# Feed-forward products of a decoder layer in a seven-product scheme, the down projection taken once for all tokens

## The chip, the core and the metric

One core of a Trainium2 chip runs the whole program. The metric is the time of one execution on the device in microseconds (us). TensorE (PE in the rows; PEld is its weight load) multiplies, VectorE (DVE), ScalarE (ACT) and GpSimd (POOL) work on elements, and SyncE (SP) issues every DMA transfer of this kernel.

## The reference

One layer for 2048 tokens of 1024 channels in float32: a token mixer, then a feed-forward block with 2816 hidden channels. Cut to what matters here:

```python
h = rmsnorm(x, norm_mix_in) * (1.0 + sc1) + sh1
q, k, v, p, u, vg = jnp.split(h @ w_in, SPLITS, axis=-1)
merged = jnp.concatenate([rmsnorm(stick_breaking_attention(q, k, v), mn[:512]),
                          rmsnorm(multiscale_pool(p), mn[512:768]),
                          rmsnorm(chunked_spatial_gating(u, vg), mn[768:])], axis=-1)
x = x + g1 * (merged @ w_out)
h2 = rmsnorm(x, norm_ffn_in) * (1.0 + sc2) + sh2
gate, up = jnp.split(h2 @ w_gate_up, 2, axis=-1)
x = x + g2 * ((jax.nn.silu(gate) * up) @ w_down)
return rmsnorm(x, final_norm)
```

The attention has 8 heads of 64 channels and looks back over 512 tokens; sc1, sh1, g1 and the like come from a conditioning vector through `w_ada`.

## The kernel before

The tokens go in four groups of 512. Every large product is made of float32 operands that are cut in a high and a low half (`a = a_hi + a_lo`, both in the format fp32r), and three products hi*hi, hi*lo and lo*hi (`mm3`) are added in PSUM. So 128 input channels by 128 output channels for 512 tokens are three matmuls with 512 columns. Cutting a weight tile (`wsplit`) costs an ACT copy and a subtraction on DVE or POOL.

- `proj_a(g)` and `proj_b(g)` make q, k, v, the pooling and the gating channels of group g. q, k and v go to scratch in DRAM.
- `attention()` is a generator. For each group and head it loads k, q and v back, and for each of four tiles of 128 queries `att_front` makes the weights: a score matmul into the PSUM tile `z`, a copy and three activations on ACT, a maximum, a prefix sum (`TENSOR_TENSOR_SCAN`) and a subtraction on DVE, masks on POOL, and the last Exp on ACT. `att_back` transposes the weights of a pair of tiles in three rounds through the one PSUM tile `tr`, cuts them (ACT, then DVE, into `wT`) and multiplies with v into `av`. After the second pair of a head, `av` goes out through a tile of its own tag (`av`, one buffer).
- `out_proj(g)` multiplies with `w_out` and adds g1 times that to x; `h_ffn(g)` transposes the normed rows into channels.
- `gate_up` makes 128 hidden channels at a time for one group: 24 matmuls for gate, 24 for up, each into one bank of the three-bank PSUM tag `d`, then the sigmoid on ACT and DVE. `down` (through `tok_gemm`) takes four hidden tiles at a time, for each of four token tiles and two halves of the channels: 12 matmuls into a bank, a DVE multiplication by g2 and a POOL addition into the rows of x held in SBUF.

The feed-forward weights are so read and cut once for each group, four times in all. The order comes from generators: `weave(fg, *sides)` emits a main generator and steps side generators and the attention at a rate per estimated microsecond; a list scheduler then sets the order on each engine from the emission order as priority, and tiles of a tag get its buffers as they come free. `hp()` raises the priority of PSUM evictions. The attention of groups 1 to 3 is stepped along with the feed-forward of groups 0 to 2 (`rate`, `limit`, `ATT_ITEMS`), and `down` of one group runs beside the start of the next.

## Time and profile before

| | |
|---|---|
| median of three runs | 2463.29 us (2462.47 to 2464.83) |
| span of the profiled execution | 2463.7 us |
| mean granted TensorE clock | 0.986 of full speed |
| busy share of PE, DVE, ACT, POOL | 95%, 69%, 55%, 49% |
| read from and written to HBM | 279.95 MB, 33.56 MB |

The profiled execution's own time is its span, from the first to the last instruction. A busy share is an average over stages with different limits: 0 to 592 us are the projections with the first output projection, and then come four feed-forward groups. Matmuls overlap in the pipeline, so the mean duration of one in the rows is longer than the time from one start to the next.

### The profile page before, as it was taken

Reading aid. Unit: us, or ns where it says so; the run is one execution under the profiler, and the core shown is the slowest. Engines: PE = TensorE matmul, PEld = TensorE weight load, DVE = VectorE, ACT = ScalarE, POOL = GpSimd, SP = SyncE. Lnnn points to the kernel's source line nnn. Section 1 sums busy time; section 2 is a strip of 40 time slices with the busy share of each in tenths; the row PEclk is TensorE's granted clock in tenths of the full one; section 3 lists DMA queues with packets and bytes.
Section 4 is the critical chain, followed back from the end, with each engine's and each line's share of the span. In section 5 each row is a group of like instructions: output and inputs, shape, how many; then the busy total and the mean of one; then the engine's idle time right before and its main releaser. Section 6 shows DMA issues by size and latency. Waiting matters only on the chain.

```text
span 2463.7 us, 32486 instructions
## 1 busy us (share of the span) xinstructions
PE 2352.7 (95%) x11730; PEld 1977.3 (80%) x11730; DVE 1692.1 (69%) x2125; ACT 1362.9 (55%) x2307; POOL 1217.0 (49%) x1157
## 2 busy tenths in 40 slices
PE   5999999999999999998999999889999999999998
PEld 4888979788788888777888888768788878788887
DVE  7577888767876777878877777877775456543435
ACT  5366767656666655656665655566664343433333
POOL 4142533345465455675554555754554456344445
PEclk8999999999999999999999999999999999999999
DMA  8857374554333333433433334334333343433332
GB/s 250 270 167 238 120 244 133 158 165 122 96 97 105 105 104 98 139 121 100 129 115 105 105 102 132 124 98 130 99 103 90 102 146 102 140 95 99 98 100 77
DMA packets 336512, 315.62 MB, mean 128 GB/s; under 512 B 12168, under 2 KB 267870, under 8 KB 336352
## 3 DMA queue, kind: packets, MB, share of 16 engines
q1 hardware_dynamic: 336352, 313.56, 41.3%
q8 instruction: 92, 1.51, 0.2%
q14 instruction: 68, 0.56, 0.1%
HBM read 279.95 MB, written 33.56 MB: 127 GB/s over the span
## 4 chain that ended last, share of the span: by engine, by line
PE 49%; DVE 18%; POOL 11%; issue 10%; ACT 8%; DMA 4%; SPq 1%; POOLq 0%; DVEq 0%; ACTq 0%
PE d L90 45%; POOL b L868 4%; DVE ee L704 3%; DVE hl L265 2%; DVE zc L707 2%; POOL hl L265 2%; PE av L90 2%; ACT hl L263 1%; DMA qst<-q_s 1%; DVE b L301 1%; PE tr L735 1%; DMA b<-in_w_ada_dram 1%; PE z L90 1%; DVE ee L690 1%; POOL b L916 1%
## 5 line engine op out<-in xcount | busy, mean ns | idle before, releaser
L90 PE MATMUL d<-b,hl 128*128 128x512 f32 x5184 | 1254.2, 395 | 8.3 <-DVE b L300 3.2
L90 PEld LDWEIGHTS d<-b,hl 128*128 128x128 f32 x5184 | 961.9, 189 | 208.2 <-DVE b L300 5.0
L90 PE MATMUL d<-hl,b 128*128 128x512 f32 (+1 forms) x4428 | 913.9, 359 | 13.2 <-DVE y L867 12.4
L90 PEld LDWEIGHTS d<-hl,b 128*128 128x128 f32 x4428 | 728.9, 191 | 128.3 <-DVE y L867 15.0
L263 ACT ACTIVATE hl<-raw 128x1024 fp32r<-128x1024 f32 x368 | 387.1, 1054 | 238.0 <-PE d L90 231.0
L265 POOL TENSOR_TENSOR hl<-raw,hl 128x1024 fp32r<-128x1024 f32 x122 | 308.2, 2527 | 325.1 <-ACT hl L263 308.7
L265 DVE TENSOR_TENSOR hl<-raw,hl 128x1024 fp32r<-128x1024 f32 x246 | 336.1, 1368 | 191.9 <-ACT hl L263 185.0
L868 POOL TENSOR_TENSOR b<-b,y 128x512 f32<-128x512 f32 x248 | 388.8, 1576 | 143.4 <-DVE y L867 135.8
L916 POOL TENSOR_TENSOR b<-y,b 128x512 fp32r<-128x512 f32 x88 | 165.0, 1875 | 228.3 <-DVE b L915 223.0
L704 DVE TENSOR_TENSOR_SCAN ee<-ee 128x640 f32<-128x640 f32 (+4 forms) x128 | 204.5, 1598 | 61.8 <-POOL ee L698 54.8
L867 DVE TENSOR_TENSOR y<-d,b 128x512 f32<-128x512 f32 x248 | 167.7, 681 | 91.4 <-PE d L90 88.9
L709 ACT ACTIVATE zc<-zc 128x640 f32<-128x640 f32 (+4 forms) x128 | 85.8, 670 | 257.5 <-POOL zc L698 223.4
L90 PE MATMUL av<-wT,vst 128*128 128x256 f32 x672 | 173.0, 295 | 30.6 <-DVE wT L751 13.4
L693 POOL TENSOR_SCALAR_AFFINE_SELECT zc<-zc 128x128 f32<-128x128 f32 x128 | 81.4, 636 | 221.9 <-DVE zc L707 213.8
L751 DVE TENSOR_TENSOR wT<-tr,wT 128x128 fp32r<-128x128 f32 (+1 forms) x280 | 116.6, 416 | 85.5 <-ACT wT L750 85.2
L90 PEld LDWEIGHTS av<-wT,vst 128*128 128x128 f32 x672 | 122.5, 192 | 59.7 <-DVE wT L751 21.4
L750 ACT ACTIVATE wT<-tr 128x128 fp32r<-128x128 f32 (+1 forms) x280 | 105.8, 378 | 104.4 <-DVE wT L751 71.2
L690 DVE SCALAR_TENSOR_TENSOR ee<-zc,ee 128x640 f32<-128x640 f32 (+4 forms) x128 | 125.5, 981 | 47.9 <-ACT ee L688 47.2
L693 POOL TENSOR_SCALAR_AFFINE_SELECT ee<-ee 128x128 f32<-128x128 f32 x128 | 53.6, 419 | 193.2 <-DVE ee L690 189.6
L907 ACT ACTIVATE y<-d 128x512 f32<-128x512 f32 x88 | 52.3, 594 | 150.8 <-PE d L90 150.7
L707 DVE TENSOR_TENSOR zc<-zc,ee 128x640 f32<-128x640 f32 (+4 forms) x128 | 133.7, 1044 | 2.4
L910 DVE SCALAR_TENSOR_TENSOR y<-d,y 128x512 f32<-128x512 f32 x88 | 60.3, 685 | 84.1 <-ACT y L909 83.7
(187 smaller groups left out, 2248.1 us busy)
## 6 DMA issues: line engine op xcount, KB each, us to landing
raw<-in_w_gate_up_dram SPq DMA_DIRECT2D x176, 512.0 KB, 3.9
raw<-in_w_down_dram SPq DMA_DIRECT2D x88, 512.0 KB, 3.7
raw<-in_w_in_dram SPq DMA_DIRECT2D x72, 512.0 KB, 5.2
b<-in_w_ada_dram SPq DMA_DIRECT2D x48, 512.0 KB, 6.7
raw<-in_w_out_dram SPq DMA_DIRECT2D x32, 512.0 KB, 4.3
b<-in_x_dram SPq DMA_DIRECT2D x28, 512.0 KB, 6.0
kst<-k_s SPq DMA_DIRECT2D x24, 512.0 KB, 4.1
qst<-q_s SPq DMA_DIRECT2D x64, 128.0 KB, 4.3
```

The source lines that it names most:

```text
L90: PE.matmul(ps, lhsT=lhsT, rhs=rhs, start=start, stop=stop)
L263: ACT.activation(out=h, in_=r, func=AF.Copy)
L265: eng.tensor_tensor(out=l, in0=r, in1=h.bitcast(F32), op=ALU.subtract)
L690: DVE.scalar_tensor_tensor(out=sp, in0=zc, scalar=0.0, in1=e, op0=ALU.max, op1=ALU.add)
L693: POOL.affine_select(out=t[:, n - P : n], in_=t[:, n - P : n], pattern=[[-1, P]], compare_op=ALU.is_ge, fill=fill, base=-1, channel_multip ...
L704: DVE.tensor_tensor_scan(out=e[:, ::-1], data0=sp[:, ::-1], data1=sp[:, ::-1], initial=0.0, op0=ALU.add, op1=ALU.bypass)
L707: DVE.tensor_tensor(out=zc, in0=zc, in1=e, op=ALU.subtract)
L750: ACT.activation(out=wT[:, 0, a:b], in_=tr[:, a:b], func=AF.Copy)
L751: DVE.tensor_tensor(out=wT[:, 1, a:b], in0=tr[:, a:b], in1=wT[:, 0, a:b].bitcast(F32), op=ALU.subtract)
L867: DVE.tensor_tensor(out=y, in0=ps, in1=gain[:, cs], op=ALU.mult)
L868: POOL.tensor_tensor(out=x1[t][:, cs], in0=x1[t][:, cs], in1=y, op=ALU.add)
L916: POOL.tensor_tensor(out=a[:, 1], in0=y, in1=a[:, 0].bitcast(F32), op=ALU.subtract)
```

## The change

- **Seven half products.** A 2x2 block product is made of seven block products in place of eight (the Winograd form of Strassen's scheme). For gate and up, one *unit* is 128 gate and 128 up channels (two block rows) for 1024 tokens (two block columns of 512), and the 1024 input channels are two block halves of four tiles. `wprep` loads the four weight blocks (`raw`), forms the sums and differences on DVE and POOL, and hands out seven cut left factors (`hl`); `build` makes the seven cut right factors `H` (28 tiles) once for each 1024 tokens; `product` is 4 x 3 matmuls, and `unit` runs seven of them over three PSUM banks `a`, `b`, `g` with partial results copied out in between (tiles `r1`, `r5`, `r2`, `r3` of the tag `y`).
- **Order.** The feed-forward now has two phases for gate and up (tokens 0 to 1023, then 1024 to 2047, 22 units each) whose activations go to DRAM (`act_s`), and then three phases for down over all tokens (8 units each, of 4, 4 and 3 hidden tiles a block) with the weights times g2 as right factors and the activations as left ones. x goes through DRAM (`x1_s`) between these phases.
- **Attention.** Groups 0 and 1 are done by the end of the projections (`limit`, `rate`), groups 2 and 3 run along with the first gate and up phase. The masks and the scan are folded, and one DVE subtraction a query tile (L707) drops out; q and v are stored already cut. The tag `zc` has two buffers in place of four, and the weights of a query tile now stand in `ee`, which has three. A head's result now leaves `av` through a tile of the tag `y`.
- **Output projection of the late groups.** `out_proj(0)` and `out_proj(1)` stand in the projections; groups 2 and 3 wait for `out_late`, between the two gate and up phases, with `w_out` held in 16 tiles and the transposes of each token tile right behind it. `build` for the second half reads its result back from DRAM (`h2_s`).
- **Buffers.** The tags `t2`, `c`, `av` and `vr` are gone into `y` (8 buffers) and `b` (28); weights are cut in halves of 512 columns.

```diff
-    BUFS = dict(vr=1, b=21, raw=3, hl=4, y=6, c=2, t2=6, sm=12, kst=1, qst=1, vst=1, zc=4, ee=3, wT=2, av=1)
+    BUFS = dict(b=28, raw=4, hl=6, y=8, sm=12, kst=1, qst=1, vst=1, zc=2, ee=3, wT=2)
...
-                            avs = st("av", [HD, 512])
-                            ACT.activation(out=avs, in_=av[HD:P, :], func=AF.Copy)
+                            avs = yt()
+                            ACT.activation(out=avs[0:HD], in_=av[HD:P, :], func=AF.Copy)
...
+    def wprep(spec):
...
+        a11, a21, a12, a22 = X[:, 0], X[:, 1], Y[:, 0], Y[:, 1]
+        t = out(a11)
+        POOL.tensor_tensor(out=a11, in0=a11, in1=a21, op=ALU.subtract)
+        DVE.tensor_tensor(out=a21, in0=a21, in1=a22, op=ALU.add)
+        yield t
+        t = out(a21)
+        DVE.tensor_tensor(out=a21, in0=a22, in1=a11, op=ALU.subtract)
+        yield t
+        t = out(a21)
+        POOL.tensor_tensor(out=a21, in0=a12, in1=a21, op=ALU.subtract)
+        yield t
...
+    def product(ps, hl, Hi, first, last=True):
+        n = len(Hi)
+        for k in range(n):
+            wh, wl = hl[:, 0, k, :], hl[:, 1, k, :]
+            hh, hlo = Hi[k][:, 0], Hi[k][:, 1]
+            mm(ps, wh, hh, first and k == 0, False, True)
+            mm(ps, wh, hlo, False, False, True)
+            mm(ps, wl, hh, False, k == n - 1, True)
+
+    def unit(left, H, done):
+
+        a = dps()
+        product(a, left(), H[0], True)
+        with hp():
+            r1 = yt()
+            ACT.activation(out=r1, in_=a, func=AF.Copy)
+        yield
+        b = dps()
+        product(b, left(), H[1], True)
+        with hp():
+            r5 = yt()
+            ACT.activation(out=r5, in_=b, func=AF.Copy)
+        yield
+        product(a, left(), H[2], False)
+        with hp():
+            r2 = yt()
+            ACT.activation(out=r2, in_=a, func=AF.Copy)
+        yield
+        product(b, left(), H[3], False)
+        with hp():
+            DVE.tensor_tensor(out=r2, in0=b, in1=r2, op=ALU.add)
+        yield
+        product(a, left(), H[4], False)
+        with hp():
+            r3 = yt()
+            ACT.activation(out=r3, in_=a, func=AF.Copy)
+            POOL.tensor_tensor(out=r5, in0=r3, in1=r5, op=ALU.add)
+        yield
+        g = dps()
+        product(g, left(), H[5], True)
+        with hp():
+            DVE.tensor_tensor(out=r1, in0=g, in1=r1, op=ALU.add)
+        yield
+        product(a, left(), H[6], False)
+        done(r1, r2, a, r5)
+        yield
...
+    def out_d(tp, last):
+        def done(c11, c12, c21, c22):
...
+                x1 = st("raw", [P, D])
+                SP.dma_start(out=x1, in_=x1_s[2 * tp + i])
...
-        rate[0] = 6.0 * ATT_ITEMS[g] / 100
+        limit[0] = min(g, 2)
+        rate[0] = 0.31 if g else 0.0
...
+            fill(5)
+            for _ in unit(left, H, fin):
+                fill(5)
...
+                if pi == 0:
+                    step(tail)
+                    credit[0] += 0.7
+                    while credit[0] >= 1.0:
+                        credit[0] -= 1.0
+                        if len(done) < limit[0]:
+                            att_step()
```

What this does to the order on the engines is shown at one place, on PE and on ACT. The first rows are of PE in the feed-forward of group 1 before: `d` are banks of the gate and up products, `z` scores, `tr` transposes of attention weights, `av` their product with v.

```order
L90 MATMUL d_11416<-b_10892,hl_11419 128x512 x2
L90 MATMUL z_11363<-kst_10996,qst_10998 128x320
L90 MATMUL av_10418<-wT_11251,vst_10415 128x256
L90 MATMUL z_11363<-kst_10996,qst_10998 128x320
L90 MATMUL av_10418<-wT_11251,vst_10415 128x256
L90 MATMUL z_11363<-kst_10996,qst_10998 128x320
L90 MATMUL av_10418<-wT_11251,vst_10415 128x256
L90 MATMUL z_11363<-kst_10996,qst_10998 128x320
L90 MATMUL av_10418<-wT_11251,vst_10415 128x256
L90 MATMUL d_11416<-b_10892,hl_11419 128x512
```

Attention stands between two matmuls of one product there, and the transposes of a round stand further on, with products around them. Next PE in the first gate and up phase of the changed kernel: `d_10839` is bank `a` of a unit, and the last row is its third product.

```order
L751 MATMUL tr_10795<-ident,ee_10575 128x128
L93 MATMUL z_10923<-kst_10672,qst_10673 128x320 x4
L93 MATMUL av_10333<-wT_10796,vst_10326 128x256 x4
L751 MATMUL tr_10809<-ident,ee_10516 128x128
L751 MATMUL tr_10809<-ident,ee_10575 128x128
L751 MATMUL tr_10809<-ident,ee_10516 128x128
L751 MATMUL tr_10809<-ident,ee_10575 128x128
L93 MATMUL av_10333<-wT_10810,vst_10326 128x256 x4
L751 MATMUL tr_10821<-ident,ee_10516 128x128
L751 MATMUL tr_10821<-ident,ee_10575 128x128 x2
L93 MATMUL av_10333<-wT_10822,vst_10326 128x256 x4
L93 MATMUL d_10839<-b_8352,hl_10720 128x512 x3
```

The three rounds of a head's last pair follow each other with no product between them. On ACT before, where a head leaves `av` (L802), in the feed-forward of group 0: L907 is the first reading of a gate bank, L908 and L909 go on with it.

```order
L687 ACTIVATE ee_8141<-ee_8141 128x640
L688 ACTIVATE ee_8141<-ee_8141 128x640
L907 ACTIVATE y_8217<-d_8157 128x512
L263 ACTIVATE hl_8403<-raw_8401 128x1024
L908 ACTIVATE y_8217<-y_8217 128x512
L909 ACTIVATE y_8217<-y_8217 128x512
L802 ACTIVATE av_8058<-av_7418 64x512
L911 ACTIVATE y_8218<-y_8218 128x512
```

And ACT of the changed kernel at the place of its PE rows above: L806 takes the head's result, L1023 and L1029 are the copies of banks `a` and `b` (`r1`, `r5`).

```order
L701 ACTIVATE ee_10749<-ee_10749 128x640
L761 ACTIVATE wT_10822<-tr_10821 128x128
L701 ACTIVATE ee_10883<-ee_10883 128x640
L702 ACTIVATE ee_10749<-ee_10749 128x640
L702 ACTIVATE ee_10883<-ee_10883 128x640
L806 ACTIVATE y_10835<-av_10333 64x512
L1023 ACTIVATE y_10852<-d_10839 128x512
L1029 ACTIVATE y_10870<-d_10857 128x512
```

The copy of bank `a` has moved behind the head's result, which takes a tile of the same tag `y` and is emitted before it.

## Rows read from the trace of the kernel before

**Rows 1.** The page's first part: busy time, share and instructions of each engine.

```profile
PE 2352.7 (95%) x11730; PEld 1977.3 (80%) x11730; DVE 1692.1 (69%) x2125; ACT 1362.9 (55%) x2307; POOL 1217.0 (49%) x1157
```

**Rows 2.** Busy time by stage: stretch, length, engines; then clock, DMA share, GB/s.

```profile
0.00:592.00 592.00, 538.85 (x3126) 469.04 (x3127) 435.16 (x597) 362.37 (x687) 240.91 (x268) 0.97 0.61 191
...
1095.00:1595.00 500.00, 482.24 (x2339) 401.78 (x2338) 387.32 (x458) 303.31 (x506) 280.51 (x289) 1.00 0.37 114
...
2065.00:2463.00 398.00, 388.75 (x1740) 321.72 (x1738) 189.58 (x236) 148.35 (x224) 178.21 (x103) 0.99 0.33 99
```

**Rows 3.** Groups on PE from 2200 to 2400 us: count | busy us, mean ns.

```profile
L90 PE MATMUL d<-b,hl 128*128 128x512 f32 x596 | 135.7, 389 | 0.0
L90 PE MATMUL d<-hl,b 128*128 128x512 f32 x288 | 65.8, 389 | 0.0
```

**Rows 4.** Groups on PE from 800 to 900 us, with attention beside the feed-forward.

```profile
L90 PE MATMUL d<-b,hl 128*128 128x512 f32 x270 | 66.9, 394 | 0.0
L90 PE MATMUL d<-hl,b 128*128 128x512 f32 x108 | 26.6, 393 | 0.0
...
L90 PE MATMUL z<-kst,qst 128*128 128x320 f32 x28 | 5.5, 308 | 0.0
```

**Rows 5.** Scans of L704, one a query tile, by stretch: DVE busy (count), clock, DMA.

```profile
0.00:592.00 592.00, 46.06 (x39) 0.97 0.61 191
...
592.00:2463.00 1871.00, 158.46 (x89) 0.99 0.36 108
```

**Rows 6.** Groups on ACT, DVE and POOL, whole run.

```profile
L709 ACT ACTIVATE zc<-zc 128x640 f32<-128x640 f32 x96 | 70.8, 737 | 223.5 <-POOL zc L698 223.4
L681 ACT ACTIVATE zc<-z 128x640 f32<-128x640 f32 x96 | 67.0, 698 | 51.1 <-PE tr L735 28.4 <-PE z L90 22.3
L907 ACT ACTIVATE y<-d 128x512 f32<-128x512 f32 x88 | 52.3, 594 | 150.8 <-PE d L90 150.7
L354 ACT ACTIVATE b<-b 128x512 fp32r<-128x512 f32 x32 | 18.8, 623 | 10.2 <-DMA b<-pg_s 6.2 <-DVE b L351 3.7
L704 DVE TENSOR_TENSOR_SCAN ee<-ee 128x640 f32<-128x640 f32 x96 | 172.0, 1791 | 55.5 <-POOL ee L698 54.8
L867 DVE TENSOR_TENSOR y<-d,b 128x512 f32<-128x512 f32 x248 | 167.7, 681 | 91.4 <-PE d L90 88.9 <-POOL b L868 2.0
L707 DVE TENSOR_TENSOR zc<-zc,ee 128x640 f32<-128x640 f32 x96 | 110.0, 1146 | 1.9
L690 DVE SCALAR_TENSOR_TENSOR ee<-zc,ee 128x640 f32<-128x640 f32 x96 | 106.9, 1114 | 36.1 <-ACT ee L688 36.0
L355 DVE TENSOR_TENSOR b<-b,b 128x512 fp32r<-128x512 f32 x32 | 25.7, 841 | 3.4 <-ACT b L354 3.4
L868 POOL TENSOR_TENSOR b<-b,y 128x512 f32<-128x512 f32 x248 | 388.8, 1576 | 143.4 <-DVE y L867 135.8
```

**Rows 7.** The page's groups for the cut of the attention weights.

```profile
L751 DVE TENSOR_TENSOR wT<-tr,wT 128x128 fp32r<-128x128 f32 (+1 forms) x280 | 116.6, 416 | 85.5 <-ACT wT L750 85.2
...
L750 ACT ACTIVATE wT<-tr 128x128 fp32r<-128x128 f32 (+1 forms) x280 | 105.8, 378 | 104.4 <-DVE wT L751 71.2
```

**Rows 8.** Waits of PE, whole run: us in total, times, longest.

```profile
PE av L90 <- DVE wT L751: 13.4, 14, 2.5
PE av L90 <- ACT wT L750: 13.2, 9, 3.6
PE d L90 <- DVE y L867: 12.4, 7, 3.8
```

**Rows 9.** DMA issues: count, KB each, median us from issue to landing.

```profile
raw<-in_w_gate_up_dram SPq DMA_DIRECT2D x176, 512.0 KB, 3.9
...
b<-a_s SPq DMA_DIRECT2D x8, 512.0 KB, 7.1
...
out_dram<-b SPq DMA_DIRECT2D x8, 256.0 KB, 2.3
```

**Rows 10.** The last matmuls in the timeline: start, length.

```profile
2434.76 21.16 PE L90 MATMUL d<-hl,b 128*128 128x512 f32 x104
```

More of the change, by code (lines that the diff above doesn't have):

```diff
@@ L153, in tile_hybrid_trunk @@
     NR = 78
-    rows = ct("rows", [NR, P])
+    rows = st("y", [NR, P])
     r0 = 0
@@ L978, in final @@
[L978 to L986 removed]
+                ACT.activation(out=e, in_=e, func=AF.Exp, scale=-1.0)
+                with hp():
+                    DVE.tensor_tensor(out=gate, in0=up, in1=gate, op=ALU.mult)
@@ L1021, in weave @@
         for e in live:
-            while e[0] is not ada and e[0] is not tail and step(e[0]):
+            while e[0] is not ada and step(e[0]):
                 pass
@@ new lines, in lefts, with fill, left @@
+    def lefts():
+        for ph in phases:
+            for spec, _ in ph[3]:
+                yield from wprep(spec)
+    stream = lefts()
+    ready = []
+    cap, made = [0], [0]
+    def fill(n):
+        while len(ready) < n and made[0] < cap[0]:
+            made[0] += 1
+            t = next(stream, None)
+            if t is None:
+                break
+            ready.append(t)
+    def left():
+        return ready.pop(0)
+    row = None
+    H = [[] for _ in range(7)]
+    for _ in build(phases[0][0], 4, None, H):
+        pass
```

663 lines of the change are left out of this document (395 added, 268 removed).

## The prediction

> **What bounds the kernel now.** I read the shares first, then stages, then single rows. PE is busy 95% of the span and no other engine more than 69% [rows 1], so PE's work sets the time; what remains is how near its stages run to PE's own pace. In a stretch with feed-forward alone, 596 + 288 = 884 matmuls of 512 columns pass in 200 us without idle time [rows 3]: 226 ns each from start to start (the 389 ns are pipelined). With attention beside it, 378 such matmuls pass in 100 us [rows 4]. They need 378 x 0.2262 = 85.5 us, and the other 14.5 us are the attention's. Its 28 score matmuls are four a query tile, so 7 tiles: 2.07 us of PE a tile. By the code the rest of the kernel after 592 us has 6336 feed-forward and 576 output projection matmuls (6912 x 0.2262 = 1563 us) and 89 tiles [rows 5] x 2.07 = 184 us, 1748 of the 1871 us; 123 us are lost, mostly at the three changes of group. The projections take 592 us [rows 2], with 39 tiles in them. PE waits little for attention or for bank readers: 13.4 + 13.2 + 12.4 us in the whole run [rows 8].
>
> **What is removed.** Feed-forward matmuls go from 4 x (44 x 24 + 44 x 12) = 6336 to 2 x 22 x 7 x 12 + 8 x 7 x 33 = 5544. The 792 fewer are 792 x 0.2262 = 179 us, all on the path while PE is the bound. The other engines do not gain as much: weights are cut twice in place of four times, but sums, partial copies and the seven factors of each side come in.
>
> **Projections, 747 us.** To the 592 us come 192 matmuls of the second output projection, 43 us, and 64 - 39 = 25 tiles of attention that are now done here, 52 us: 687 us. The order adds idle time. In three places PE has the transposes and products of about four query pairs (36 transposes, 46 products with v and 32 scores in the longest) and no projection matmul between them; before there is none such. Eight tiles cost ACT 4 x 0.737 + 0.698 + 105.8/128 = 4.5 us each [rows 6, 7], 36 us, against 17 us of PE: some 20 us of waiting each, 60 us. Bounds: nothing, if the other engines run ahead, and 100 us.
>
> **First gate and up phase, 646 us.** PE: 22 units x 84 matmuls = 1848 x 0.2262 = 418 us, and the other 64 tiles x 2.07 = 132 us, 550 us. Can the others keep up? ACT has per unit 7 cuts, 4 bank copies and 6 sigmoid steps, 17 x about 0.62 us = 10.5 us [rows 6], with the tiles 22 x 10.5 + 64 x 4.5 = 519 us of durations. DVE has per unit 4.2 cuts and 2 sums at 0.84, 2 bank additions at 0.68 and 6 steps at 0.7 us, 10.8 us, and a tile 1.79 + 1.11 + 116.6/128 = 3.8 us [rows 6, 7] (the 1.15 us of L707 is gone, off PE's path): 22 x 10.8 + 64 x 3.8 = 481 us. Both are under 550 us, but not by much.
>
> What I do not take as hidden are the bursts in the order. Once a head, 16 times here, a unit has its three banks full (`a`, `b`, `g` each with a product done), and its third product must wait until ACT has copied `a`. That copy now stands behind the taking of the head's result, because both want a buffer of `y` and the head's was asked for first. So PE runs the last pair's three rounds bare. A round is transposes, an ACT copy of 0.4 to 0.6, a DVE subtraction of 0.4 to 0.7 (the upper ends by L907 and L867) [rows 6, 7] and four products, 2.3 to 2.8 us with the handoffs, 7 to 8.4 us for three; ACT has up to five steps of 0.74 us between them. PE's own work in it is some 3 us. So it stands 4 to 9 us; I take 6, being nearer to the chain without delays, since ACT's steps partly lie ahead: 16 x 6 = 96 us. Bounds: 0, as the stretch of rows 4 shows attention with no PE idle, and 16 x 15 = 240 us if each burst also waits for a whole new tile on ACT, DVE and POOL.
>
> A DVE subtraction of 512 columns takes 0.68 us with one operand in PSUM and 0.84 us with both in SBUF, while POOL is busy half the time [rows 1, 6]: contention costs it 0.16 us on average. The Trainium skill, in "SBUF — State Buffer", section "Who interferes with whom", says more: DVE with two SBUF inputs and a POOL operation that reads SBUF shut each other out for a whole instruction. By the row the 481 us stand; by that rule at its worst, with each of the unit's 6.2 such DVE operations behind a POOL operation, DVE would be the bound of this phase. That is a rival below.
>
> **Late output projection, 104 us, and the gap behind it, 20 us.** 384 x 0.2262 = 87 us, 64 transposes 7 us, and 10 us at its start, where `w_out` and the merged rows want the `b` buffers that the last unit's `H` frees one product at a time. Behind it nothing can cover PE: the second half's factors need the last token tile. The chain is two DVE steps (0.68 + 0.84), the norm on ACT and DVE and the transposes, some 5 us (an estimate from rows 6), a store of 2.3 us and a load of 3.9 to 7.1 us [rows 9], and a first cut of 0.62 + 0.84: 14 to 18 us, and 20 us with the slower clock that follows idle PE (0.97 in the stage with the most, 1.00 without [rows 2]).
>
> **Second gate and up phase, 423 us; down, 443 us.** Each is 1848 matmuls, 418 us. Without attention the other engines have room (10.5 and 10.8 us of ACT and DVE for 19 us of PE), and the bank copies have one product, 2.7 us, to be done: 5 us for the 28 cuts of `H` at the start, at 4 x 0.62 us against 2.7 us a product. For down I add 25 us. Units of the last part are 14.2 us, and the chain addition (2.1) - norm (3.4) - freed `raw` buffer - load (3.9) - cut (1.5) is 10.9 us against about 12; the three builds and this chain may show 0 to 50 us.
>
> **The end, 8 us.** PE ends at 2434.76 + 21.16 = 2455.9 us now, 7.8 us before the end [rows 10]; most of the last unit's sums are ready before its last product, so the tail keeps its length.
>
> Sum: 747 + 646 + 104 + 20 + 423 + 443 + 8 = **2391 us**, against a span of 2463.7, which is 0.4 us over the median of the runs. That is 2.9% less.
>
> **Rivals.**
> - *The bursts are covered.* For: attention lies beside the feed-forward with PE at 100.00 of 100 us in the window of rows 4. Against: there the attention is half as dense. Without the 96 us and with 15 of the 60 us: 2250 us. Chance 0.27.
> - *The burst is the whole attention chain.* Each head's last pair waits for a tile just started, 15 us in place of 6, and the three long runs 40 in place of 20: 2391 + 144 + 60 = 2595 us, slower. It decides from 72/16 = 4.5 us more a burst. For: the scan alone is 1.8 us and ACT's wait for POOL's mask 223 us in all [rows 6]. Against: PE's longest waits for `wT` now are 2.5 and 3.6 us [rows 8]. Chance 0.15.
> - *DVE and POOL shut each other out.* 22 x 6.2 DVE operations each 1.58 us late [L868, rows 6] are 215 us: 481 + 215 = 696 in place of 646 us, 2441 us. The skill's page named above has this rule; the mean of 0.84 us speaks against its worst case. Chance 0.08.
> - *The seven products wait for their banks*, so that the scheme does not save what it cuts. There are 44 x 7 + 24 x 7 = 476 products; 0.3 us each is 143 us and 2534 us, and 0.15 us ends the gain. Against: 2.7 us of cover and bank waits of 12.4 us now. Chance 0.05.
> - *My forecast*, 2340 to 2450 us: chance 0.45.
>
> **Range and chances.** 2270 to 2475 us leaves out the lower part of the first rival and the two slow ones. Differences under 0.2% (5 us) this measurement can't tell from none. Faster: nearly all of the forecast, the first rival and most of the third, 0.78; the same 0.04; slower 0.18.
>
> **What would show it.** Right: the feed-forward groups on PE hold 5544 matmuls; from the second gate and up phase on, 1848 pass in about 420 us, PE idle near nothing; in the first, PE's idle time lies at `d`, released by ACT's copy L1023, and at `av`, released by `wT`, some 100 us together; one gap of 15 to 20 us before the second phase, ended by the cuts of `H`. Wrong: that idle time under 30 us or over 200, products waiting in the second phase, or a down phase over 480 us.

## The result, and the profile after

The change makes the kernel slower: 2926.57 us (median of four, 2920.56 to 2930.07) against 2463.21 us, a ratio of 1.1876 with a 95% interval of 1.1859 to 1.1893. The profiled execution has a span of 2925.6 us. The page's first part, beside [rows 1]:

```profile
PE 2432.1 (83%) x10926; PEld 1958.5 (67%) x10926; DVE 1764.4 (60%) x2283; ACT 1492.4 (51%) x2862; POOL 1366.4 (47%) x1500
```

PE has fewer instructions than in [rows 1] and is busy longer, in part because its granted clock is lower, 0.879 of full speed in the mean in place of 0.986. No engine is the bound any more. By stage (columns as in [rows 2]; the bounds are the starts of each phase's first matmul: projections, first gate and up phase, late output projection with the gap behind it, second gate and up phase, down):

```profile
0.00:927.00 927.00, 742.14 (x3952) 618.05 (x3952) 563.78 (x797) 521.03 (x1048) 409.99 (x570) 0.87 0.55 174
927.00:1765.00 838.00, 672.56 (x2817) 532.19 (x2818) 499.17 (x666) 496.08 (x919) 394.27 (x537) 0.82 0.28 84
1765.00:1929.00 164.00, 125.51 (x463) 91.66 (x461) 63.28 (x99) 45.59 (x98) 21.15 (x15) 0.85 0.38 126
1929.00:2390.00 461.00, 435.85 (x1848) 353.38 (x1848) 294.66 (x346) 227.37 (x411) 228.88 (x162) 0.96 0.29 88
2390.00:2917.00 527.00, 455.50 (x1847) 363.10 (x1848) 339.81 (x373) 200.65 (x387) 312.11 (x219) 0.93 0.45 151
```

| stage | forecast | measured | difference |
|---|---|---|---|
| projections | 747 | 927 | +180 |
| first gate and up phase | 646 | 838 | +192 |
| late output projection and gap | 104 + 20 | 164 | +40 |
| second gate and up phase | 423 | 461 | +38 |
| down | 443 | 527 | +84 |
| end | 8 | 8 | 0 |

Every stage but the end is longer than forecast, the two with attention by 372 of the 534 us; how much of that is the attention's is asked of a run without it below. The second phase and down hold no attention and still miss PE's 418 us.

**One stretch of the first gate and up phase**, PE in the timeline (start, length, what; in brackets the idle time before, and what ended it):

```profile
1201.32 0.38 PE L751 MATMUL tr<-ident,ee 128*128 128x128 f32 x2
1204.49 0.85 PE L93 MATMUL z<-kst,qst 128*128 128x320 f32 x4 [2.79 <-ACT zc L696]
1206.74 0.48 PE L751 MATMUL tr<-ident,ee 128*128 128x128 f32 x1 [1.39 <-ACT ee L725]
...
1211.80 1.73 PE L93 MATMUL av<-wT,vst 128*128 128x256 f32 x4 [0.69 <-ACT wT L761]
...
1216.41 0.82 PE L93 MATMUL av<-wT,vst 128*128 128x256 f32 x2 [0.47 <-ACT wT L761]
1217.03 0.63 PE L751 MATMUL tr<-ident,ee 128*128 128x128 f32 x2
1219.43 8.45 PE L93 MATMUL d<-b,hl 128*128 128x512 f32 x29 [1.78 <-ACT y L1023]
```

For 18 us no product runs. The stretch ends as predicted, when ACT has copied bank `a` (L1023). But it holds more than the three rounds that I had counted: a score matmul waits for ACT to empty `z` into a `zc`, and the first transpose waits for the last Exp (L725). The weights were not ready; the whole chain of a pair runs here. There are 16 such stretches in this phase, one a head, 5 to 33 us long and 290 us together (counted in the timeline as times of over 5 us without a product; one more, of 5.7 us at 978, holds a wait of the norm and no pair). The waits of PE in the phase name the same places:

```profile
PE z L93 <- ACT zc L696: 56.0, 22, 5.0
PE av L93 <- ACT wT L761: 37.1, 53, 1.6
...
PE tr L751 <- ACT ee L725: 11.1, 10, 4.0
...
PE d L93 <- ACT y L1023: 7.7, 5, 1.8
```

**The pace of a pair with nothing beside it** is read best in the projections, 604 to 658 us, where PE has no product at all. ACT there; L700 is the first activation that takes an `ee`, L761 the first half of the cut of a round:

```profile
605.25 0.74 ACT L700 ACTIVATE ee<-zc 128x640 f32<-128x640 f32 x1 [2.69 <-PE tr L751]
...
616.17 0.27 ACT L761 ACTIVATE wT<-tr 128x128 fp32r<-128x128 f32 x1
...
619.50 0.60 ACT L761 ACTIVATE wT<-tr 128x512 fp32r<-128x512 f32 x1 [2.32 <-PE tr L751]
...
622.19 0.74 ACT L700 ACTIVATE ee<-zc 128x640 f32<-128x640 f32 x1 [2.10 <-PE tr L751]
...
622.84 0.36 ACT L761 ACTIVATE wT<-tr 128x256 fp32r<-128x256 f32 x1
...
639.15 0.74 ACT L700 ACTIVATE ee<-zc 128x640 f32<-128x640 f32 x1 [2.10 <-PE tr L751]
```

A pair of query tiles begins every 16.95 us, and each time L700 waits for a transpose, the third round's: the next pair's activations seem to find an `ee` only when the pair before has been transposed (a run with one more `ee` asks that below). From L700 on, two pairs do not overlap. Beside products the rounds themselves are slower. The same cuts (first, second and third round) in the covered stretch that follows the one above:

```profile
1228.03 0.28 ACT L761 ACTIVATE wT<-tr 128x128 fp32r<-128x128 f32 x1 [0.55 <-PE tr L751]
...
1234.94 0.60 ACT L761 ACTIVATE wT<-tr 128x512 fp32r<-128x512 f32 x1 [1.24 <-PE tr L751]
...
1242.32 0.36 ACT L761 ACTIVATE wT<-tr 128x256 fp32r<-128x256 f32 x1
```

Rounds are 6.9 and 7.4 us apart here and 3.3 us in the bare stretch, so a pair beside products should take some 10 us more, 27 us (an estimate from these spacings). The scans of this phase bear it out: from pair to pair they are mostly 17 to 20 us apart where a bare stretch lies between and 25 to 30 us where it doesn't. That is nearly the 7 tiles in 100 us of [rows 4], 28.6 us a pair.

### The profile page after: what moved, and what is told of

It reads as the page before. It is cut to its first block, busy times and chain, and to the rows that moved or that the text cites. A ratio compares the mean times of both kernels' runs of the same rounds, so it can differ in the third digit from the quotient of the medians.

```text
span 2925.6 us, 32946 instructions
## 1 busy us (share of the span) xinstructions
PE 2432.1 (83%) x10926; PEld 1958.5 (67%) x10926; DVE 1764.4 (60%) x2283; ACT 1492.4 (51%) x2862; POOL 1366.4 (47%) x1500
## 5 line engine op out<-in xcount | busy, mean ns | idle before, releaser
L93 PE MATMUL d<-b,hl 128*128 128x512 f32 x6504 | 1632.2, 409 | 179.3 <-ACT hl L271 48.9
L93 PEld LDWEIGHTS d<-b,hl 128*128 128x128 f32 x6504 | 1267.5, 198 | 490.4 <-ACT hl L271 57.2
L267 POOL TENSOR_TENSOR hl<-raw,hl 128x512 fp32r<-128x512 f32 (+1 forms) x262 | 370.6, 1416 | 476.4 <-ACT hl L271 450.9
L271 ACT ACTIVATE hl<-raw 128x512 fp32r<-128x512 f32 (+1 forms) x652 | 392.4, 617 | 388.2 <-PE d L93 153.9
L267 DVE TENSOR_TENSOR hl<-raw,hl 128x512 fp32r<-128x512 f32 (+1 forms) x390 | 346.3, 896 | 169.0 <-ACT hl L271 162.9
L93 PE MATMUL d<-hl,b 128*128 128x256 f32 (+1 forms) x1920 | 303.1, 312 | 11.5 <-DVE y L870 5.7
L93 PEld LDWEIGHTS d<-hl,b 128*128 128x128 f32 x1920 | 267.5, 194 | 32.6 <-DVE y L870 6.2
L715 DVE TENSOR_TENSOR_SCAN ee<-ee,zc 128x640 f32<-128x640 f32 (+4 forms) x128 | 191.7, 1498 | 23.8 <-POOL ee L707 21.0
L93 PE MATMUL z<-kst,qst 128*128 128x320 f32 (+1 forms) x448 | 117.4, 379 | 86.1 <-ACT zc L696 77.3
L707 POOL TENSOR_SCALAR_AFFINE_SELECT zc<-zc 128x128 f32<-128x128 f32 x128 | 77.8, 608 | 226.6 <-DVE ee L704 226.5
L761 ACT ACTIVATE wT<-tr 128x128 fp32r<-128x128 f32 (+1 forms) x280 | 105.4, 377 | 121.1 <-PE tr L751 100.3
L707 POOL TENSOR_SCALAR_AFFINE_SELECT ee<-ee 128x128 f32<-128x128 f32 x256 | 145.3, 572 | 44.7 <-DVE ee L715 43.6
L751 PE MATMUL tr<-ident,ee 128*128 128x128 f32 x560 | 124.5, 327 | 26.7 <-ACT ee L725 26.6
L725 ACT ACTIVATE ee<-ee 128x640 f32<-128x640 f32 (+4 forms) x128 | 83.8, 668 | 120.2 <-POOL zc L694 58.4
L704 DVE SCALAR_TENSOR_TENSOR ee<-zc,ee 128x640 f32<-128x640 f32 (+4 forms) x128 | 105.7, 842 | 40.2 <-ACT ee L702 40.2
```

The costliest lines, as they stand in the source:

```text
L93: PE.matmul(ps, lhsT=lhsT, rhs=rhs, start=start, stop=stop, skip_group_check=skip)
L267: eng.tensor_tensor(out=dst, in0=src, in1=hi.bitcast(F32), op=ALU.subtract)
L271: ACT.activation(out=dst[:, 0], in_=src, func=AF.Copy)
L704: DVE.scalar_tensor_tensor(out=e, in0=zc, scalar=0.0, in1=e, op0=ALU.min, op1=ALU.subtract)
L707: POOL.affine_select(out=t[:, n - P : n], in_=t[:, n - P : n], pattern=[[-1, P]], compare_op=ALU.is_ge, fill=fill, base=-1, channel_multip ...
L715: DVE.tensor_tensor_scan(out=e[:, ::-1], data0=e[:, ::-1], data1=zt[:, 1 : n + 1][:, ::-1], initial=0.0, op0=ALU.add, op1=ALU.subtract,)
```

## The experiments

Two theories stood at the start. TIE is that of the prediction: a unit's third product waits behind the head's result in tag `y`. CHAIN: the attention is one chain, a pair after the other, and whatever the order is, PE must stand bare for the pairs that don't fit beside products. The stage times of all runs that gave a full split, from their timelines (us; P projections, G1 and G2 the two gate and up phases, C late output projection and gap, D down):

| run | total | P | G1 | C | G2 | D |
|---|---|---|---|---|---|---|
| changed kernel | 2926.57 | 927 | 838 | 164 | 461 | 527 |
| own tag for the result | 2922.37 | 918 | 842 | 167 | 461 | 525 |
| four `hl` (control) | 2959.08 | 939 | 838 | 163 | 472 | 537 |
| control, `zc` 4, `ee` 4 | 2850.08 | 889 | 778 | 161 | 476 | 537 |
| the same, own tag | 2829.09 | 885 | 761 | 165 | 475 | 533 |
| control, `ee` 4 | 2852.61 | 887 | 785 | 162 | 475 | 534 |
| control, `zc` 4 | 2956.06 | 932 | 846 | 162 | 475 | 531 |
| three heads early | 2933.80 | 987 | 790 | 159 | 463 | 525 |
| no masks | 2854.87 | 894 | 797 | 165 | 464 | 524 |
| low halves on DVE | 2849.73 | 904 | 830 | 157 | 450 | 497 |
| cuts and builds on DVE | 2825.38 | 905 | 830 | 157 | 434 | 490 |
| no g2 in the builds | 2892.74 | 925 | 839 | 164 | 452 | 504 |
| deep, own tag, DVE | 2706.73 | 855 | 737 | 156 | 452 | 496 |
| the same, sums on DVE | 2701.10 | 857 | 726 | 159 | 450 | 499 |
| eight products | 2855.89 | 921 | 804 | 156 | 487 | 479 |
| eight, deep, own tag, DVE | 2721.73 | 855 | 741 | 154 | 484 | 479 |
| no attention | 2278.09 | 663 | 462 | 158 | 464 | 521 |
| eight, no attention | 2285.78 | 662 | 491 | 158 | 485 | 480 |

Each is one execution, beside the kernel before at 2460.91 to 2463.52 us. The changed kernel's own four runs span 9.5 us, so differences of less than some 10 us are read as none.

### The tie, or the chain

```diff
-                            avs = yt()
+                            avs = st("av", [P, 512])
```

(`y` has seven buffers of 512 columns then, `av` one.)

> The head's result gets a tag of its own, paid for with one y buffer. Theory TIE (PE waits because a unit's third product needs the copy of bank a, which stands behind the head's result in tag y): the bare stretches go, 16 in the first gate and up phase at some 14 us of idle time each and the three in the projections, so about 2927 - 224 - 100 = 2600 us. Theory CHAIN (the attention is one chain of dependent steps, 16.9 us a pair of query tiles even when PE does nothing else, because the next pair finds no free buffer in ee and zc; 64 pairs are 1085 us of it alone): the waiting only moves to other places, in fewer and longer stretches, and the total stays at 2927 +- 60 us.

2922.37 us: TIE falls. The bare stretches are not gone, they have moved together. The windows of this run, in order a stretch with products, a bare one, and both again:

```profile
917.00:1192.00 275.00, 248.65 (x1122) 202.03 (x1123) 207.92 (x258) 175.66 (x326) 151.72 (x170) 0.94 0.29 88
1192.00:1358.00 166.00, 91.02 (x299) 66.23 (x298) 70.38 (x95) 85.69 (x159) 57.73 (x121) 0.54 0.21 62
1358.00:1584.00 226.00, 223.39 (x1057) 185.71 (x1056) 161.91 (x212) 150.47 (x281) 125.20 (x145) 0.99 0.33 99
1584.00:1728.00 144.00, 73.14 (x235) 52.09 (x233) 56.03 (x78) 66.50 (x125) 42.80 (x91) 0.53 0.21 64
```

The two bare stretches hold attention's matmuls and no product; 166 + 144 = 310 us take the place of the 290 us in 16 pieces. They also show the clock: 0.94 and 0.99 beside products, 0.54 and 0.53 without. And they show the pace. The scans (L715, two a pair) in the same four stretches, the first from where the attention begins; DVE busy (count), clock:

```profile
974.00:1192.00 218.00, 25.89 (x15) 0.99 0.30 92
1192.00:1358.00 166.00, 30.95 (x20) 0.54 0.21 62
1358.00:1584.00 226.00, 23.50 (x14) 0.99 0.33 99
1584.00:1728.00 144.00, 23.11 (x15) 0.53 0.21 64
```

Beside products a pair comes every 29 and 32 us, in the bare stretches every 17 and 19 us.

Next the buffers, with four `hl` in place of six to pay for them. The control:

```diff
-    BUFS = dict(b=28, raw=4, hl=6, y=8, sm=12, kst=1, qst=1, vst=1, zc=2, ee=3, wT=2)
+    BUFS = dict(b=28, raw=4, hl=4, y=8, sm=12, kst=1, qst=1, vst=1, zc=2, ee=3, wT=2)
...
-            fill(5)
+            fill(3)
```

> Control for the next one: four hl buffers in place of six and three factors made ahead in place of five, nothing else. Both theories: 2927 +- 40 us; a phase without attention must show whether the shorter lead costs anything.

On it `zc` and `ee`, and then the own tag as well:

```diff
-    ... zc=2, ee=3, wT=2)
+    ... zc=4, ee=4, wT=2)
```

> As the control, with the freed 8 KB in zc (4 in place of 2) and ee (4 in place of 3), so that a second pair can start while the first is still being transposed. TIE: the bare stretches stay where they are, a few us shorter: 2850 to 2927. CHAIN: the period of a pair in a bare stretch falls from 16.9 to 10 to 12 us, and projections plus first gate and up phase lose 150 us or more: 2650 to 2780 us.

```diff
-    ... y=8, sm=12, kst=1, qst=1, vst=1, zc=4, ee=4, wT=2)
+    ... y=7, sm=12, kst=1, qst=1, vst=1, zc=4, ee=4, wT=2, av=1)
...
-                            avs = yt()
+                            avs = st("av", [P, 512])
```

> Both: own tag for the head's result, and four buffers each of zc and ee, with four hl. TIE: as with the own tag alone, 2600. CHAIN: as with the deeper buffers alone, within 60 us of that run.

The control costs 32 us, 21 of them in the two stages without attention. Against it the deeper buffers give 109 us, 110 of them in P and G1 (1777 to 1667). That is CHAIN's direction but less than its 150. The time itself, 2850.08 us, lies at the lower end of TIE's range, which was set against 2927 us; against the control the gain is more than the 77 us that range allowed. With the own tag as well it is 130 us, within CHAIN's 60 us of the run before and far from TIE's 2600. Which of the two tags it was:

```diff
-    ... zc=2, ee=3, wT=2)
+    ... zc=2, ee=4, wT=2)
```

> Four ee buffers in place of three on the control with four hl (2959 us), zc at two. If ee binds (the activations L700 of the next pair wait for the last transposes of the pair before, 2 us each time in the bare stretches): most of the 109 us, 2850 to 2890. If zc binds: 2930 to 2959.

```diff
-    ... zc=2, ee=3, wT=2)
+    ... zc=4, ee=3, wT=2)
```

> Four zc buffers in place of two on the control with four hl (2959 us), ee at three. If zc binds (the score's copy L696 waits for the scan of the pair before): 2850 to 2890. If ee binds: 2930 to 2959.

One more `ee` gives 106 us, two more `zc` give 3. So it is the tag in which the weights now stand. The pairs with four `ee`, ACT in a stretch nearly without products as above:

```profile
609.79 0.74 ACT L700 ACTIVATE ee<-zc 128x640 f32<-128x640 f32 x1 [2.68 <-PE tr L751]
...
622.93 0.74 ACT L700 ACTIVATE ee<-zc 128x640 f32<-128x640 f32 x1 [1.61 <-PE tr L751]
...
636.54 0.74 ACT L700 ACTIVATE ee<-zc 128x640 f32<-128x640 f32 x1 [2.10 <-PE tr L751]
...
652.58 0.74 ACT L700 ACTIVATE ee<-zc 128x640 f32<-128x640 f32 x1 [0.73 <-PE tr L751]
```

They begin 13.1, 13.6 and 16.0 us apart in place of 16.95, not the 10 to 12 us that CHAIN expected, and L700 still waits for transposes.

Two runs ask the chain in other ways. One starts group 2's first three heads ahead of the first build:

```diff
+                if g == 2 and h == 2:
+                    pend()
+                    pend = None
+                    yield ("done", "early")
...
-        limit[0] = min(g, 2)
+        limit[0] = g
...
+    need("early")
     for _ in build(phases[0][0], 4, None, H):
```

> The changed kernel with three heads of group 2 done ahead of the first build, where the attention otherwise pauses (no scan between about 830 and 960 us); nothing left out. CHAIN: the first gate and up phase has 13 heads in place of 16 at 53 us each, 160 us less, and the projections take 40 to 80 us more, so 2810 to 2890 us. TIE or an engine's load as the bound: the bare stretches only move, 2927 +- 30 us.

2933.80 us, a miss for CHAIN and inside the 2927 +- 30 of its rival: G1 lost 49 us and P gained 60. The early heads came to stand in bare stretches of their own around the end of P (19 and 34 us, and 18 right behind the first products of G1), so starting sooner is no gain where no product lies beside. The other leaves the four masks of a tile out:

```diff
-        diagonal(zc, 0.0)
-        diagonal(e, 0.0)
...
-        diagonal(e, NEG)
-        if g > 0:
-            POOL.affine_select(
...
```

> The changed kernel with the four masks of a query tile left out (two POOL steps of 0.57 us ahead of the scan and two behind it; the weights are then those without the causal and window limits). CHAIN: 2.3 us less a tile, up to 4.6 us a pair where the two tiles' masks follow each other on POOL, so the pair's period alone falls from 16.9 to 12 to 14.5 us, and 64 pairs give 150 to 290 us: 2640 to 2780. If PE, ACT or DVE is what the attention waits for: POOL has room (47% busy), and the time falls by less than 40.

The period alone fell to 13.98 us (L700 at 625.25, 639.23), as CHAIN said, but the total by only 72 us, half of its lower bound and nearly twice what its rival allowed. 72 / 2.97 is 24, so the shorter chain pays for about 24 of the 64 pairs (an estimate); they would be those that run bare, while the others follow PE's order between products. So CHAIN holds for the bare pairs, and the expectation was wrong in taking all pairs as bare.

### What the attention costs, and what the scheme is worth

Both kernels without attention; the body of the loop over heads becomes one copy:

```diff
             for h in range(NH):
...
+                SP.dma_start(out=a_s[g][h * HD : (h + 1) * HD, :], in_=k_s[g][h][0])
+                yield
```

> The changed kernel without attention: each head's result is a copy of k, all else as it was (the whole attention is left out). CHAIN: the projections take their PE work, about 592 - 39 x 2.07 + 43 = 554 us and up to 30 more, the first gate and up phase about 425 us like the second one, and the rest what it took (131 + 24 + 460 + 527 + 8), in sum about 2140 us. Rival SCHEME (the seven products with their banks, copies and cuts wait by themselves): the first gate and up phase stays over 550 us.

> The kernel before without attention, in the same way. PE bound: 2463 - 128 x 2.07 = 2198 us, or some 50 less if the waits at the changes of group were the attention's. With the run above this gives what the scheme is worth by itself: 179 us less by the count of matmuls, less the builds.

2278.09 and 2164.23 us, the second between its two expectations. Attention costs the kernel before 2463 - 2164 = 299 us, near its 265 us of PE time, and the changed one 2927 - 2278 = 649. Of the 464 us, 350 are so the attention's. The other 114 are not: without any attention the changed kernel is still slower, with 792 fewer matmuls. Its windows (first gate and up phase, second, down):

```profile
663.00:1125.00 462.00, 437.96 (x1860) 354.77 (x1861) 286.40 (x365) 234.13 (x426) 216.62 (x156) 0.96 0.30 95
...
1283.00:1747.00 464.00, 436.19 (x1849) 353.39 (x1850) 290.50 (x347) 227.94 (x411) 228.70 (x162) 0.96 0.28 88
1747.00:2268.00 521.00, 452.41 (x1848) 360.93 (x1848) 342.80 (x373) 199.84 (x386) 312.51 (x219) 0.93 0.46 153
```

Neither of the two expectations held in full: G1 is 462, not 425, but far from 550, and the total is 138 us over CHAIN's 2140, of which 79 or more are in the projections, 663 where 554 to 584 were expected. To see what the scheme itself does, the next kernels keep order, phases and builds and take eight plain products (four cut blocks on each side, bank copies instead of sums):

```diff
+        for i, j in ((0, 0), (2, 0), (0, 2)):
+            ps = dps()
+            product(ps, L[i], H[j], True, False)
+            yield
+            product(ps, L[i + 1], H[j + 1], False)
```

> The same order, phases, buffers and builds with eight products in place of seven (four cut left and four right factors, three copies of a bank a unit in place of four and the sums), nothing left out. Theory ORDER (the order costs the time, by the attention and the builds, and the scheme is worth its matmuls): 792 more, 179 us of PE, of which those beside the attention only fill bare stretches; builds with 16 cuts in place of 28; in all 2927 + 0 to 100. Rival SCHEME (the cuts, copies and sums of the seven products are what the attention and the builds wait for): under 2850 us.

And the same with the copy in place of the attention:

> Eight products and no attention (left out as in the run of the seven without it, 2278 us). If the seven products save their 179 us of matmuls in a quiet pipeline: 2278 + 179 - 60 for shorter builds = about 2400. If the builds and the sums eat the gain: first and second gate and up phase about 490 each, down about 480, in sum 2260 to 2300.

Eight products are faster than seven, 2855.89 us, six over what SCHEME named and well under ORDER's range. Without attention the two are 8 us apart, 2285.78 and 2278.09, the second case of its expectation. Eight products, the same three phases:

```profile
662.00:1153.00 491.00, 486.75 (x2134) 400.49 (x2135) 160.10 (x229) 188.63 (x340) 82.21 (x62) 1.00 0.30 96
...
1311.00:1796.00 485.00, 482.10 (x2114) 398.26 (x2114) 158.67 (x199) 175.80 (x312) 102.08 (x72) 0.99 0.29 90
1796.00:2275.00 479.00, 478.46 (x2111) 395.86 (x2110) 144.62 (x185) 135.09 (x255) 115.65 (x85) 1.00 0.49 158
```

2112 x 0.2262 = 478 us is PE's own time, and down takes 479: its builds are hidden. With seven products PE's own time is 418 and down takes 521, DVE has 342.80 us of work in place of 144.62 and POOL 312.51 in place of 115.65. Of 179 us saved on PE, 171 are lost again, most of it in down, where seven products are slower than eight. The other 2286 - 2164 = 122 us of the eight without attention are the order's (phases of 1024 tokens with a gap ahead of the second, x and the activations through DRAM). The traces split them by stage. The first gate and up matmul starts at 550.5 us in the kernel before without attention and at 662 here; 43 of these 111 us are the second output projection, so the projections lose 68. The late output projection with its gap takes 158 us for 87 us of matmuls and loses 71. The feed-forward itself loses 23 us here and some 38 in the kernel before, at its changes of group. What in the new order costs the projections their 68 us no run shows.

### Where the builds lose it

In the last unit before a phase the `build` has 28 low halves, 16 differences and, for down, 16 multiplications by g2; 29 are on DVE, 31 on POOL. DVE and then POOL in such a build of the changed kernel, timeline:

```profile
2553.14 1.77 DVE L267 TENSOR_TENSOR b<-kst,b 128x512 fp32r<-128x512 f32 x1
2554.84 1.77 DVE L267 TENSOR_TENSOR b<-vst,b 128x512 fp32r<-128x512 f32 x1
2556.54 0.68 DVE L1091 TENSOR_TENSOR kst<-kst 128x512 f32<-128x512 f32 x1
2557.14 0.68 DVE L1091 TENSOR_TENSOR vst<-vst 128x512 f32<-128x512 f32 x1
2557.74 1.79 DVE L267 TENSOR_TENSOR b<-zc,b 128x512 fp32r<-128x512 f32 x1
```

```profile
2552.63 1.74 POOL L267 TENSOR_TENSOR b<-qst,b 128x512 fp32r<-128x512 f32 x1
2554.32 1.74 POOL L267 TENSOR_TENSOR hl<-raw,hl 128x512 fp32r<-128x512 f32 x1
2557.29 1.68 POOL L1097 TENSOR_TENSOR kst<-ee,kst 128x512 f32<-128x512 f32 x1 [1.23 <-DVE kst L1091]
```

A subtraction of two SBUF tiles of this size takes 0.68 us while POOL is idle (2556.54) and 1.77 while it works (2553.14), and it ends half a microsecond after POOL's does, as if it had waited for it. One of each takes 1.70 us.

```diff
-        eng = POOL if cnt[0] % 5 in (1, 3) else DVE
+        eng = DVE
```

> All low halves of the cuts on DVE, none on POOL (two of five were). Theory PORT (a DVE subtraction of two SBUF tiles, 0.68 us, and a POOL operation, 1.3 us, run one after the other, 1.77 us for the two; in the builds both engines are full and exclude each other): a cut costs 0.68 us of the common port in place of 0.93, the three builds of the down phase and the one ahead of the second gate and up phase get shorter, down 527 to about 480 us, in sum 2927 - 40 to 80 us. Rival LOAD (the engines run side by side and DVE is merely busy): DVE gets 262 x 0.7 = 180 us more and the builds get longer, down over 540 us, 2940 to 3000 us.

With that, the builds' own operations (four such lines for the rows, one for the differences):

```diff
-                POOL.tensor_tensor(out=xl, in0=xl, in1=row[:, 0:512], op=ALU.mult)
+                DVE.tensor_tensor(out=xl, in0=xl, in1=row[:, 0:512], op=ALU.mult)
...
-            POOL.tensor_tensor(out=XR[q], in0=B[q], in1=XR[q], op=ALU.subtract)
+            DVE.tensor_tensor(out=XR[q], in0=B[q], in1=XR[q], op=ALU.subtract)
```

> All low halves on DVE, and the builds' multiplications by g2 and their differences on DVE too; nothing left out. PORT: a build of the down phase has 28 low halves, 16 differences and 16 multiplications, of them 31 on POOL; one after the other they are 29 x 0.68 + 31 x 1.3 = 60 us beside 19 us of products, and all on DVE 60 x 0.68 = 41 us; so each of the three builds gets about 20 us shorter, down 527 to 467, in sum about 2790 to 2850 us. LOAD (separate engines, DVE the later one): DVE's 41 us in place of 20 make each build longer, down over 540 us.

And on the changed kernel alone:

```diff
-                nxt = build(nsrc, nn, row if nscaled else None, nH)
+                nxt = build(nsrc, nn, None, nH)
```

> The multiplication of w_down's rows by g2 left out (so the down product lacks g2), all else as it was. PORT: 16 POOL operations of 1.3 us less a build, 21 us, three times: down 527 to 465 to 480 us, total 2865 to 2885. Rival: the builds wait for the loads or for ACT's 28 copies of 0.62 us, 17 us, less than the 19 us of a unit: nothing changes, 2927 +- 15.

Low halves on DVE: 77 us less, inside PORT's range, with down at 497; only 41 of them lie in G2 and D, and 23 in the projections, where weights are cut too. With the builds on DVE too it is 101 us. Down is 490 and not 467; but the first of the three builds lies in the last unit of G2, and G2 and D together lose 64 us, which is 21 a build. Without g2, PORT expected 42 to 62 and got 34. So PORT holds in sign and, for the move to DVE, in size; LOAD falls. In this run G2 takes 434 us, 53 less than with eight products (whose cuts are still on both engines), so there most of the 60 us that the scheme saves on PE in a phase arrive; in down, at 490 against 479, they still do not. A second face of the port shows in what is left, though how much of it that explains is not shown. POOL in a build of the run with cuts and builds on DVE, where DVE follows one subtraction by the next:

```profile
2513.66 7.07 POOL L1001 TENSOR_TENSOR raw<-raw,raw 128x512 f32<-128x512 f32 x1 [13.26 <-DVE hl L267]
```

One POOL difference of the left factors, 1.3 us elsewhere, took 7.07 us, and it ended only after ten such DVE operations. ACT's cut of that factor waited for it, and PE for the cut. ACT there, then PE there and ahead of it:

```profile
2520.76 2.71 ACT L271 ACTIVATE hl<-raw 128x512 fp32r<-128x512 f32 x5 [5.31 <-POOL raw L1001]
```

```profile
2474.70 27.57 PE L93 MATMUL d<-b,hl 128*128 128x512 f32 x120
...
2513.63 4.63 PE L93 MATMUL d<-b,hl 128*128 128x512 f32 x10 [2.27 <-DVE hl L267]
2521.44 2.26 PE L93 MATMUL d<-b,hl 128*128 128x512 f32 x4 [3.17 <-ACT hl L271]
```

Between the waits the matmuls start 427 ns apart, where 227 are usual (their starts in the trace); the granted clock from 2510 to 2530 us is 0.51, the lower of its two levels (1.2 GHz in place of 2.4).

Three runs put parts together: the deep buffers and own tag (with four `hl`) with the cuts and builds on DVE; the sums too, of which two are shown:

```diff
-        POOL.tensor_tensor(out=a11, in0=a11, in1=a21, op=ALU.subtract)
+        DVE.tensor_tensor(out=a11, in0=a11, in1=a21, op=ALU.subtract)
...
-            POOL.tensor_tensor(out=r5, in0=r3, in1=r5, op=ALU.add)
+            DVE.tensor_tensor(out=r5, in0=r3, in1=r5, op=ALU.add)
```

and eight products with buffers of their own:

```diff
-    BUFS = dict(b=28, raw=4, hl=6, y=8, sm=12, kst=1, qst=1, vst=1, zc=2, ee=3, wT=2)
+    BUFS = dict(b=25, raw=4, hl=6, y=8, sm=12, kst=1, qst=1, vst=1, zc=4, ee=5, wT=2, av=1)
```

> The deeper buffers with the own tag for the head's result, and all of the cuts and builds on DVE. If the two gains are separate they add up: 2829 - 80 to 130 = 2700 to 2750 us. Still slower than 2463, since the attention stays one chain in the projections and the first gate and up phase.

> As the run with deeper buffers and all cuts and builds on DVE (2707 us), with the weights' differences, the sum of r3 and r5 and the last addition of a down unit on DVE too; nothing left out. PORT: POOL no longer waits for gaps of DVE (there single POOL operations took 4 and 7 us), down 496 to about 450, second gate and up phase 452 to 430, total 2620 to 2670. LOAD: DVE then has some 16 us a unit of 19 and beside the attention too much: the first phase gets longer by 50 or more and the total over 2720.

> Eight products with four zc, five ee and an own tag for the head's result (b has 25 buffers, as eight products need fewer right factors), cuts and builds on DVE; nothing left out. The gains of the parts were 71 (eight), 109 to 130 (deeper buffers), 77 to 101 (DVE): if they add up, 2640 to 2680 us, a little under the seven's 2707. If the seven's sums were the loss that the DVE version already took away: 2720 to 2780.

The gains add up, 2706.73 us. The last sums on DVE change 6 us, which is none: PORT's 2620 to 2670 is missed, and so is LOAD's over 2720. D does not move, though POOL no longer has the operations that took 4 and 7 us. That fits DVE as the builds' bound by then (it is busy for 17.99 of 20 us in the build shown above) and was not asked further. Eight products with much the same fixes (five `ee` in place of four, six `hl`) come to 2721.73, the second case of their expectation: the gains of the parts do not add, and eight and seven are within 1% again. No version came near 2463.

## Why the prediction was wrong

The matmuls were counted rightly (6504 - 960 = 5544 in the feed-forward), the bare stretches were at the places named, and the gap ahead of the second phase (24 us for 20) and the end (8) were sized nearly rightly. One of its own signs of being wrong came: a down phase of 527 us, over 480. The idle time of the first phase did not lie where it said either: PE's waits at `d` for L1023 and at `av` for `wT` are 7.7 + 37.1 = 45 us in place of some 100, and the largest is at `z`, 56 us.

Of the 536 us between forecast and result, 228 are the attention's: it costs 649 us, where the forecast's terms for it are 39 x 2.07 + 52 + 60 + 132 + 96 = 421. The other 308 stand without any attention, in 2278 us where the rest of the forecast is 1970: 109 in the projections (663 for 554), 44 in the first phase (462 for 418), 34 in the late output projection, 41 in the second phase and 78 in down, and 2 by rounding and at the end. What failed, by its steps:

- **"So it stands 4 to 9 us; I take 6."** Measured: 18 us without a product in the mean, and PE idle or slow through it. The step took the weights as ready and counted the three rounds alone. But front and rounds of a pair follow each other: the weights now stand in `ee` until their last transpose, and `ee` has three buffers for pairs of two. The fact stood in the description of the change, and I priced only the DVE step that it removes. One buffer more is worth 106 us (`ee` 4, against its control). The rival that a burst is the whole chain had 15 us and the right mechanism; its 2595 us stayed far short, since it left the other stages as they were.
- **The cause named for the wait was not it.** The tag `y` decides where PE stands, not how long in all: with a tag of its own the stretches moved and the total did not.
- **The density of the attention.** "Against: there the attention is half as dense" was the reading that counted: [rows 4] show 28.6 us a pair beside products. Without attention the projections and the first phase end at 1125 us, with PE's 265 us for it at 1390; 64 pairs would need one every 22 us. Beside products they come at 27 to 32, so about half ran bare at 17 to 19. The sums for ACT (519 us) and DVE (481) in the first phase were near the rows, 496 and 499; they bounded the engines' work and said nothing of a chain through all of them.
- **"The projections take 592 us."** The base was cut too early, and so is the boundary that the description of the stages gives: the last group's projection, 192 matmuls of 256 columns, follows the first output projection in the kernel before, and its first gate and up matmul starts at 616.69 us. So 25 us of projections were missing from the 747, and stood in the 123 us put down to the changes of group. PE of the kernel before, around the boundary:

```profile
615.65 1.20 PE L90 MATMUL d<-hl,b 128*128 128x256 f32 x8
616.69 3.59 PE L90 MATMUL d<-b,hl 128*128 128x512 f32 x15
```

- **The clock had no term.** I took 226 ns a matmul everywhere but in one gap. In the first phase the granted clock is 0.82, in the projections 0.87 in place of 0.97. What it costs the products can be counted from their starts: behind each bare stretch some 512-column matmuls start 427 ns apart before the spacing falls to 227, in the first phase 151, which is 30 us, and in the whole run 438, 87 us (13 us in the kernel before). Of the 192 us the first phase is over, 122 are PE busy for longer and 165 - 96 = 69 more idle time; but most of the 122 is not the products'. With the own tag, where the bare stretches lie together, PE is busy in them for 91 + 73 = 164 us with 35 tiles of attention, priced at 35 x 2.07 = 72. The stage's mean clock does not give the cost. 550 / 0.82 = 671 us happens to meet the row's 672.56, but with the own tag the mean is 0.80, which would give 687, and PE is busy for less in a phase as long:

```profile
918.00:1760.00 842.00, 664.60 (x2819) 527.53 (x2819) 518.83 (x667) 495.25 (x921) 395.74 (x538) 0.80 0.28 85
```

- **The builds.** 25 us for three of them, and 5 for the second phase. Without attention, down is 521 - 418 = 103 us over PE's time and the second phase 46. The step looked at ACT's 28 copies and not at DVE and POOL, which exclude each other: 60 operations, 29 x 0.60 + 31 x 1.26 = 56 us by their spacings (an estimate), beside 19 us of products. The rule of the Trainium skill that stands in the prediction ("SBUF — State Buffer", section "Who interferes with whom": DVE with two SBUF inputs and a GpSimd operation that reads SBUF block each other for an instruction) agrees with the rows above, 0.68 against 1.77 us. I had set it against a mean of 0.84 us, which mixes operations with and without a neighbour on POOL, and looked for it in the first phase alone.
- **"All on the path while PE is the bound."** Without attention 8 of the 179 arrived, no more than the spread of runs. This was the rival that the products wait for something of their own, at 0.05, but for the most part not for their banks: for factors and builds, 101 of the 171 lost in down.
- **The late output projection.** 164 us against 124: its 384 matmuls ran at a clock of 0.85 between stops of some 4.6 us, one behind each token tile, in which PE transposes and waits for ACT and DVE in turn. I had not seen them.

What is not settled: why the rounds stand 7 us apart beside products (PE's fixed order, or the copies and subtractions that queue on ACT and DVE; eight products with their lighter DVE load shortened the first phase by 34 us, which speaks for the second in part), what in the order makes the projections some 68 us longer, and what holds down at 490 us once the builds are on DVE.

## What to carry to other kernels

A saving on the busiest engine is worth what the others can feed: price the scheme's sums and cuts per unit on DVE and POOL together, as one resource where both read two SBUF tiles, and at the point where they come in a burst. A chain of dependent steps has a pace of its own; divide the time that will be left beside it by the number of its steps before packing it closer, and count the buffers of the tile that lives longest. Idle time of PE is paid a second time in the clock, here 87 us of products at the lower level. Check, too, where a stage of the kernel before really ends, by the first matmul of the next.

## What the runs showed of the hardware

A DVE subtraction of two 128x512 SBUF tiles took 0.68 us alone and 1.77 us beside POOL; where DVE followed one by the next every 0.60 us, a POOL operation of 1.3 us took 7.07 us, ten DVE operations long. The granted clock was 0.53 to 0.54 over whole stretches of 144 and 166 us in which PE ran attention alone, busy for 73 and 91 us of them, and 512-column matmuls behind waits started 427 ns apart in place of 227.
